# Norms with 1/rms kept in PSUM, squares added one tile late, biases on ScalarE, and other banks and held weights in the output products

## The chip, the cores and the metric

The kernel runs on one core of a Trainium2 chip. The metric is the device time of one execution in microseconds. Five engines work side by side, each on a queue of its own in program order: TensorE (PE in the profile) for matmuls, VectorE (DVE), ScalarE (ACT), GpSimd (POOL), and SyncE (SP), which issues most DMAs. They meet through semaphores. TensorE writes its products to banks of PSUM; the kernel's tiles there hold 128 x 512 fp32 numbers (a `wide` one is two of them), and a tile's place is written anew once its last reader is through.

## What is computed

The reference is one step of a diffusion backbone of two layers on 128 prompt tokens and 512 latent tokens, with 1024 features. Cut to what matters here:

```python
for l in range(DEPTH):
    hp = modulate(rmsnorm(xp, norm_mix_g[l]), sp_m, sc_m)
    hs = modulate(rmsnorm(xs, norm_mix_g[l]), ss_m, scs_m)
    # even layer: SSD scan and attention, @ w_out; odd layer: RG-LRU, @ w_out
    xp = xp + gp_m * out_p
    xs = xs + gs_m * out_s
    xp = xp + gp_f * conv_ffn(modulate(rmsnorm(xp, norm_ffn_g[l]), sp_f, sc_f), *fw)
    xs = xs + gs_f * conv_ffn(modulate(rmsnorm(xs, norm_ffn_g[l]), ss_f, scs_f), *fw)
def rmsnorm(x, g):
    return x * lax.rsqrt(jnp.mean(x * x, axis=-1, keepdims=True) + EPS) * g
def modulate(h, shift, scale):
    return h * (1.0 + scale) + shift
def conv_ffn(h, w_up, conv_w, conv_b, w_down):
    u = dwconv_centred(h @ w_up, conv_w, conv_b)
    val, g = jnp.split(u, 2, axis=-1)
    return (jax.nn.silu(g) * val) @ w_down
```

Shift, scale and gate (the modulation) come from a product of two conditioning vectors with `w_mod`. All is fp32.

## The kernel before

**Layout.** Activations lie transposed: features on the 128 partitions in 8 tiles (KD = 8), tokens in 644 columns (128 prompt, 4 empty, 512 latent). Each fp32 product is made of three matmuls on operands that are split in a high and a low part (`mm3`, lines 470 to 472): high by high, low by high, high by low. So every weight is loaded by DMA (`wraw`, three buffers), cast by ScalarE to its high part (line 112) and subtracted by GpSimd in pieces of 256 columns for its low part (line 117). These standard slots hold three weights. In the last products of a stage further weights are "held": they are split into a pool of their own (lines 126 and 129) that is opened when buffers of the stage before are given back. In the FFN most up weights come in pairs whose sums and differences VectorE makes (lines 139 to 142).

**Order.** The order on each engine is that of the program. It is written by hand: every product of one weight tile counts as a tick, and `after(n, f)` puts f n ticks later. NORM_A, NORM_B, NORM_D and NORM_F say after how many ticks the steps of a norm come.

**Output products.** `out_parts` (line 644) makes the eight tiles of an output product, first for the columns of part 0 and then of part 1 (388 and 256 columns, in B 260 and 384). Each tile is read from PSUM by VectorE, times the gate, and added to the residual X (`add_part`, line 317 as X<-..., the helper `fma`). `bank` or `wide_banks` hands out the PSUM banks: in A two of 512 columns in turn (tag "g"), elsewhere three pairs. Weights are split ahead by AHEAD = 3, but no further than the eighth. This is used four times: A is layer 0's output product (line 1440), B and D the last down products of the two FFNs (line 1636), C that of the RG-LRU (line 1852).

**Norms.** `square_acc` (lines 533 to 537) squares each new tile of X on ScalarE and adds the square on VectorE to `sq`. When a part is done, `norm_part` puts into the stream of products: the sums over features by TensorE (line 554), mean and eps by VectorE (line 556), the power -1/2 by GpSimd (line 558), a product that spreads 1/rms of a token over all partitions (line 565), and ScalarE's copy of it from PSUM to `sq` (line 569). Then `gen` makes tile after tile: VectorE multiplies 1/rms, the scale and X (`fma`, one operation for each stream of tokens), ScalarE adds the shift (line 600) and casts to the high part `hhi` (line 603; for even tiles lines 600 and 603 are one operation). `low` makes the low part `hlo`: for odd tiles by GpSimd (line 69), for even ones by VectorE, which adds the shift again (`fma`). In the two FFN norms the rows are kept (`keep`, `k.full`). From them `sums` (lines 1498 to 1502) makes the sums for paired weights; there VectorE first adds the shift to the even tiles, and GpSimd makes one of four differences.

**Modulation.** `make_mod` spreads the product with `w_mod` over the first half of the kernel, up to 1108 us. Each `M.step` (line 332, eight small matmuls) writes a PSUM bank that VectorE adds to `macc` (lines 338 and 340); after eight steps two transposes (line 347) and VectorE's line 352 finish a part. `small()` (line 545) gives the bank: where the plan of PSUM is "narrow" always "m", else `mtile()` hands out "m" and "o" in turn. FFN 0 isn't narrow and has 45 such steps; the norms' sums and rows take their banks from `mtile()` too.

## Time and profile before

| | us |
|---|---|
| median of 3 runs | 2131.27 |
| lowest, highest | 2123.99, 2131.78 |
| the profiled execution | 2128.0 |
| its span, first to last instruction | 2126.2 |

The profiled execution took 1.8 us more than its span. By stretches of the span:

| stretch | us | TensorE busy | VectorE busy | clock |
|---|---|---|---|---|
| 720 to 801.4 (A, output products of layer 0) | 81.4 | 70.08 | 38.56 | 0.96 |
| 801.4 to 860 (head of FFN 0) | 58.6 | 48.56 | 46.76 | 0.90 |
| 860 to 1272 (FFN 0) | 412.0 | 403.87 | 313.15 | 0.99 |
| 1272 to 1322.3 (B, last down products of FFN 0) | 50.3 | 35.34 | 34.92 | 0.87 |
| 1322.3 to 1550 (RG-LRU) | 227.7 | 179.50 | 188.84 | 0.87 |
| 1550 to 1617.6 (C, output products of the RG-LRU) | 67.6 | 52.62 | 39.17 | 0.85 |
| 1617.6 to 1680 (head of FFN 1) | 62.4 | 48.89 | 46.31 | 0.86 |
| 1680 to 2069 (FFN 1) | 389.0 | 372.73 | 302.76 | 0.99 |
| 2069 to 2126.2 (D, last down products and outputs) | 57.2 | 40.73 | 27.77 | 0.90 |

Busy times are in us. The clock is the mean that was granted to TensorE, 1.00 for the higher of its two levels (2.4 GHz) and 0.50 for the lower (1.2 GHz). TensorE is busy 1891.4 us in all (89%), VectorE 1467.3 (69%), GpSimd 1208.1 (57%) and ScalarE 964.2 (45%). Where TensorE's busy time is near the stretch's length, the products set the time; elsewhere what ends its idle time does.

### The profile page before, as it was taken

Reading aid. Unit: us, or ns where it says so; the run is one execution under the profiler, and the core shown is the slowest. Engines: PE = TensorE matmul, PEld = TensorE weight load, DVE = VectorE, ACT = ScalarE, POOL = GpSimd, SP = SyncE. Lnnn points to the kernel's source line nnn. Section 1 sums busy time; section 2 is a strip of 40 time slices with the busy share of each in tenths; the row PEclk is TensorE's granted clock in tenths of the full one; section 3 lists DMA queues with packets and bytes.
Section 4 is the critical chain, followed back from the end, with each engine's and each line's share of the span. In section 5 each row is a group of like instructions: output and inputs, shape, how many; then the busy total and the mean of one; then the engine's idle time right before and its main releaser. Section 6 shows DMA issues by size and latency. Waiting matters only on the chain.

```text
span 2126.2 us, 33767 instructions
## 1 busy us (share of the span) xinstructions
PE 1891.4 (89%) x12665; PEld 1735.7 (82%) x12665; DVE 1467.3 (69%) x2486; ACT 964.2 (45%) x1671; POOL 1208.1 (57%) x1542
## 2 busy tenths in 40 slices
PE   6878889999999988999999997977778799999997
PEld 4767768888888878799889997977678799999986
DVE  3477755656664357687777876788857778777874
ACT  3454444454553334343333444766724444343445
POOL 3335454333343535466666775688755577766772
PEclk9889999999999999999999998989789899999998
DMA  9545432121113431444542222111111122222221
GB/s 267 165 156 164 149 110 63 49 54 48 49 45 124 131 117 64 136 130 153 178 145 70 60 84 79 53 39 45 40 50 41 37 79 82 86 76 70 60 85 65
DMA packets 255578, 196.60 MB, mean 92 GB/s; under 512 B 13837, under 2 KB 233816, under 8 KB 255288
## 3 DMA queue, kind: packets, MB, share of 16 engines
q1 hardware_dynamic: 252664, 184.59, 28.9%
q0 software_dynamic: 2528, 7.13, 1.4%
q8 instruction: 100, 1.64, 0.3%
q10 hardware_dynamic: 224, 2.73, 0.3%
q14 instruction: 62, 0.51, 0.1%
HBM read 187.50 MB, written 6.92 MB: 91 GB/s over the span
## 4 chain that ended last, share of the span: by engine, by line
PE 36%; DVE 11%; POOL 9%; ACT 4%; issue 4%; DMA 4%; POOLq 0%; DVEq 0%; ACTq 0%; SPq 0%
PE wide L470 10%; PE wide L471 10%; PE wide L472 10%; POOL t L69 4%; POOL wlo L117 4%; DMA wraw<-in_ffn_w_up_dram 4%; DVE ft L317 2%; PE mt L332 1%; PE gh L470 1%; DVE X L317 1%; PE gh L471 1%; PE gh L472 1%; DVE wsum L141 1%; DVE wraw L140 1%; DVE wsum L139 1%
## 5 line engine op out<-in xcount | busy, mean ns | idle before, releaser
L117 POOL TENSOR_TENSOR wlo<-wraw,whi 128x256 fp32r<-128x256 f32 (+1 forms) x845 | 715.7, 875 | 544.7 <-ACT whi L112 476.8
L470 PE MATMUL wide<-hhi,whi 128*128 128x322 f32 (+4 forms) x1072 | 352.5, 329 | 49.5 <-DVE X L317 23.0
L471 PE MATMUL wide<-hlo,whi 128*128 128x322 f32 (+4 forms) x1072 | 345.8, 323 | 3.7 <-DVE hlo L511 3.4
L472 PE MATMUL wide<-hhi,wlo 128*128 128x322 f32 (+4 forms) x1072 | 343.1, 320 | 0.0
L112 ACT CAST whi<-wraw 128x1024 fp32r<-128x1024 f32 (+2 forms) x263 | 220.1, 839 | 150.4 <-PE wide L472 71.9
L470 PEld LDWEIGHTS wide<-hhi,whi 128*128 128x128 f32 x1072 | 213.2, 199 | 66.4 <-issue 21.6
L470 PE MATMUL gh<-hhi,whi 128*128 128x322 f32 (+3 forms) x704 | 236.7, 336 | 9.1 <-ACT zt L1160 8.6
L471 PE MATMUL gh<-hlo,whi 128*128 128x322 f32 (+3 forms) x704 | 221.2, 314 | 1.3 <-DVE hlo L511 1.0
L472 PE MATMUL gh<-hhi,wlo 128*128 128x322 f32 (+3 forms) x704 | 220.5, 313 | 0.0
L471 PEld LDWEIGHTS wide<-hlo,whi 128*128 128x128 f32 x1072 | 212.6, 198 | 6.1 <-DVE hlo L511 5.3
L472 PEld LDWEIGHTS wide<-hhi,wlo 128*128 128x128 f32 x1072 | 212.4, 198 | 0.0
L470 PE MATMUL wide<-hidh,whi 128*128 128x322 f32 (+4 forms) x624 | 199.7, 320 | 2.2 <-DVE ft L1584 2.2
L471 PE MATMUL wide<-hidl,whi 128*128 128x322 f32 (+4 forms) x624 | 195.5, 313 | 1.6 <-DVE hidl L511 1.6
L472 PE MATMUL wide<-hidh,wlo 128*128 128x322 f32 (+4 forms) x624 | 195.4, 313 | 0.0
L317 DVE SCALAR_TENSOR_TENSOR ft<-ft,PC 128x643 f32<-128x643 f32 x160 | 168.2, 1072 | 37.3 <-ACT ft L1526 35.3
L470 PEld LDWEIGHTS gh<-hhi,whi 128*128 128x128 f32 (+1 forms) x704 | 134.0, 190 | 34.7 <-issue 21.3
L1526 ACT ACTIVATE ft<-ft,PC 128x644 f32<-128x644 f32 x80 | 74.0, 927 | 144.4 <-DVE ft L1591 133.4
L317 DVE SCALAR_TENSOR_TENSOR X<-wide,modc,X 128x128 f32<-128x128 f32 (+3 forms) x264 | 123.5, 511 | 19.8 <-PE wide L472 19.8
L471 PEld LDWEIGHTS gh<-hlo,whi 128*128 128x128 f32 (+1 forms) x704 | 133.8, 190 | 2.4 <-DVE hlo L511 1.2
L472 PEld LDWEIGHTS gh<-hhi,wlo 128*128 128x128 f32 (+1 forms) x704 | 133.6, 190 | 0.6
L470 PEld LDWEIGHTS wide<-hidh,whi 128*128 128x128 f32 x624 | 118.7, 190 | 15.9 <-issue 7.0
L112 ACT CAST shi<-wsum 128x512 fp32r<-128x512 f32 x120 | 72.8, 617 | 124.3 <-DVE wsum L141 111.4
(386 smaller groups left out, 4676.4 us busy)
## 6 DMA issues: line engine op xcount, KB each, us to landing
wraw<-in_ffn_w_up_dram SPq DMA_DIRECT2D x88, 512.0 KB
mraw<-in_w_mod_dram SPq DMA_DIRECT2D x80, 512.0 KB
wraw<-in_ssd_attn_w_in_dram SPq DMA_DIRECT2D x42, 512.0 KB
wraw<-in_ffn_w_down_dram SPq DMA_DIRECT2D x96, 192.0 KB
E<-ad SPq DMA_DIRECT2D x16, 640.0 KB
mraw<-in_w_mod_dram SPq DMA_DIRECT2D x32, 256.0 KB
wraw<-in_ssd_attn_w_out_dram SPq DMA_DIRECT2D x16, 512.0 KB
wraw<-in_lru_w_in_dram SPq DMA_DIRECT2D x16, 512.0 KB
```

The costliest lines, as they stand in the source:

```text
L69: getattr(eng, op)(out[:, c], a[:, c], b[:, c])
L112: self.nc.scalar.copy(hi, src)
L117: low.tensor_sub(lo[:, q], src[:, q], hi[:, q].bitcast(F32))
L139: v.tensor_sub(s[:, 1], a[:, :4], b[:, :4])
L140: v.tensor_add(b[:, :4], b[:, :4], b[:, 4:])
L141: v.tensor_sub(s[:, 0], b[:, :4], a[:, :4])
L317: nc.vector.scalar_tensor_tensor(out, in0, scalar, in1, op0=op0, op1=op1, **kw)
L332: nc.tensor.matmul(m[32 * j:32 * j + 32, :256], scp[:, kt, :], raw[:, j * 256:(j + 1) * 256], start=half is None or kt == 0, stop=half is ...
L470: nc.tensor.matmul(ps[:whi.shape[-1], p0:p0 + c1 - c0], whi, xhi[:, c0:c1], start=start, stop=False)
L471: nc.tensor.matmul(ps[:whi.shape[-1], p0:p0 + c1 - c0], whi, xlo[:, c0:c1], start=False, stop=False)
L472: nc.tensor.matmul(ps[:whi.shape[-1], p0:p0 + c1 - c0], wlo, xhi[:, c0:c1], start=False, stop=stop)
L1526: after(at, lambda: nc.scalar.activation(out, u, AF.Identity, scale=par(cw, 2 * NF + t), bias=par(cb, t)))
```

## The change

1. The rows of 1/rms stay in PSUM, in bank "o"; `gen` reads them there (`box.m`), and ScalarE's copies go. The norm of the SSD output keeps the copies.
2. `square_acc` adds the square of the tile before, instead of its own; `rstd_cols` adds the last one.
3. With `keep`, every tile gets its shift on ScalarE in place and is then cast; the low part of an even tile is one subtraction on VectorE. The additions of shifts in `sums` go, and GpSimd's difference moves to VectorE.
4. In A, two of three pairs of tiles get wide banks.
5. The number of weights in standard slots is given for each of the four places: 2 in A (six held), 0 in B (eight held), 3 in C and D as before. The bound at the eighth weight goes, so that the next stage's first weights are split during part 0 if slots are free.
6. `small()` and `rstd_cols` always take bank "m".

```diff
@@ -40,7 +40,7 @@
 FF_CHUNKS = (3, 3, 3, 3, 3, 3, 4)
 N_PLAIN = 2
 PIECE = 256
-N_STD = 3
+N_STD = (2, 0, 3, 3)
 N_WAIT = 1
 AHEAD = 3
 N_HID, N_FT = 4, 5
@@ -392,7 +392,7 @@
             add_w(w_in, 0, 8, b + 128 * h)
     for half in range(2):
         for n in range(8):
-            add_w(w_out, 1024 * half, 8, 128 * n, kind=held(n, N_STD) if half else None)
+            add_w(w_out, 1024 * half, 8, 128 * n, kind=held(n, N_STD[0]) if half else None)
 
     def early(c):
         return 1 if c else FF_CHUNKS[c]
@@ -412,7 +412,7 @@
 
         def downs(c, last=False):
             for n in range(8):
-                add_w(dn, 128 * starts[c], FF_CHUNKS[c], 128 * n, kind=held(n, N_STD) if last else None)
+                add_w(dn, 128 * starts[c], FF_CHUNKS[c], 128 * n, kind=held(n, N_STD[1 + 2 * l]) if last else None)
         for c, n in enumerate(FF_CHUNKS):
             ups(c, 0, early(c))
             if c:
@@ -543,11 +553,12 @@
         return k.psum.tile([128, 512], F32, name="mt", tag=tag, bufs=1)
 
     def small():
-        return mtile("m" if k.narrow else None)
+        return mtile("m")
 
     def rstd_cols(chunks):
 
-        m = mtile()
+        add_square()
+        m = mtile("m")
         n = len(chunks)
         for i, c in enumerate(chunks):
             c0, c1 = CHUNKS[c]
@@ -558,19 +569,15 @@
         nc.gpsimd.tensor_tensor(r, v, expo[:, :n], op=OP.pow)
         return r
 
-    def rstd_rows(r, hf):
-
-        m = mtile()
+    def rstd_rows(r, hf, tag):
+
+        m = mtile(tag)
         for i in range(len(k.cut.chunks[hf])):
             nc.tensor.matmul(m[:, 128 * i:128 * i + 128], r[:, i:i + 1].to_broadcast([128, 128]), ident,
                              start=True, stop=True)
-        at = 0
-        for _, c0, c1 in k.cut.segs[hf]:
-            nc.scalar.copy(k.sq[:, c0:c1], m[:, at:at + c1 - c0])
-            at += c1 - c0
+        return m
 
     def norm_part(hf, l, which, keep=None, then=None, at=NORM_B):
-
 
         box, ts = Core(), {}
         k.fresh[hf] = False
@@ -581,9 +588,12 @@
 
         def low(kt):
             t, h, lo = ts.pop(kt), hhi[kt], hlo[kt]
-            if kt % 2:
+            if kt % 2 or keep:
                 c = slice(*k.cut.parts[hf])
-                pieces(nc.gpsimd, "tensor_sub", lo[:, c], t[:, c], h[:, c].bitcast(F32))
+                if kt % 2:
+                    pieces(nc.gpsimd, "tensor_sub", lo[:, c], t[:, c], h[:, c].bitcast(F32))
+                else:
+                    nc.vector.tensor_sub(lo[:, c], t[:, c], h[:, c].bitcast(F32))
                 return
             for s, c0, c1 in segs:
                 B = modc[l][:, s, 24 * which + kt:24 * which + kt + 1]
@@ -594,11 +604,13 @@
                 t = ts[kt] = keep[kt] if keep else k.tmp.tile([128, NT], F32, name="sqt", tag=k.sq_tag, bufs=k.n_sqt)
                 if hf == 0 and (kt % 2 or keep):
                     nc.vector.memset(t[:, NP:S0], 0.0)
+                whole, at = kt % 2 or keep, 0
                 for s, c0, c1 in segs:
                     A, B = acol[l][which][:, s, kt:kt + 1], modc[l][:, s, 24 * which + kt:24 * which + kt + 1]
-                    fma(t[:, c0:c1], k.sq[:, c0:c1], A, X[:, kt, c0:c1], op0=OP.mult, op1=OP.mult)
-                    nc.scalar.activation((t if kt % 2 else hhi[kt])[:, c0:c1], t[:, c0:c1], AF.Identity, bias=B)
-                if kt % 2:
+                    fma(t[:, c0:c1], box.m[:, at:at + c1 - c0], A, X[:, kt, c0:c1], op0=OP.mult, op1=OP.mult)
+                    nc.scalar.activation((t if whole else hhi[kt])[:, c0:c1], t[:, c0:c1], AF.Identity, bias=B)
+                    at += c1 - c0
+                if whole:
                     c = slice(*k.cut.parts[hf])
                     nc.scalar.copy(hhi[kt][:, c], t[:, c])
             if kt:
@@ -608,7 +620,10 @@
                 then()
 
         after(at[0], cols)
-        after(at[0] + at[1], lambda: rstd_rows(box.r, hf))
+        def rows():
+            box.m = rstd_rows(box.r, hf, "o")
+
+        after(at[0] + at[1], rows)
         for kt in range(KD + 1):
             after(at[0] + at[1] + at[2] + at[3] * kt, lambda kt=kt: gen(kt))
 
@@ -641,7 +656,7 @@
                     M.step()
                     W.ahead()
 
-    def out_parts(xs, evac, then, banks, first, ready, n_std=N_STD):
+    def out_parts(xs, evac, then, banks, first, ready, n_std):
 
 
         ws, base = [], W.next
@@ -668,7 +683,7 @@
                 for j, f in enumerate(late):
                     f()
                     if j == len(late) - 1:
-                        W.upto(min(base + batch[-1][-1] + AHEAD, base + 7))
+                        W.upto(base + batch[-1][-1] + AHEAD)
                         break
                     for g in batch:
                         for i in g:
@@ -1369,7 +1384,10 @@
 
             def rows(rs):
                 for hf in range(2):
-                    rstd_rows(rs[hf], hf)
+                    m, at = rstd_rows(rs[hf], hf, "m"), 0
+                    for _, c0, c1 in k.cut.segs[hf]:
+                        nc.scalar.copy(k.sq[:, c0:c1], m[:, at:at + c1 - c0])
+                        at += c1 - c0
                 for t in range(KD):
                     after(5 * t + 5, lambda t=t: fma(X[:, t], X[:, t], par("ssd_g", t), k.sq, op0=OP.mult, op1=OP.mult))
             after(5 * KD + 8, lambda: after(12, lambda rs=[rstd_cols(c) for c in k.cut.chunks]: rows(rs)))
@@ -1412,7 +1430,14 @@
                 k.given.clear()
             half_unit(H, out, ready=lambda c0: k.n or c0 in k.given, cuts=k.cut.parts if k.n == 7 else HALVES)
 
+        turn = []
+
         def bank(n):
+
+            if n == 2:
+                turn.append(0)
+            if n == 2 and len(turn) % 3:
+                return wide_banks(2)
             return [k.psum.tile([128, 512], F32, name="gh", tag="g", bufs=2) for _ in range(n)]
 
         def ready():
@@ -1437,7 +1462,7 @@
                 until(lambda: k.fresh[0])
         until(lambda: len(k.given) == 2)
         hctx = ExitStack()
-        out_parts(H, evac, then, bank, [[0], [1]], [ready])
+        out_parts(H, evac, then, bank, [[0], [1]], [ready], N_STD[0])
         W.over = None
         hctx.close()
 
@@ -1492,12 +1517,8 @@
             def sums(kt):
 
                 x, y = full[kt], full[kt + 4]
-                if kt % 2 == 0:
-                    for i, t in ((kt, x), (kt + 4, y)):
-                        for s, cols in STREAMS:
-                            nc.vector.tensor_scalar(t[:, cols], t[:, cols], modc[l][:, s, 24 + i:25 + i], None, op0=OP.add)
                 nc.vector.tensor_sub(x[:, L], x[:, R], x[:, L])
-                nc.gpsimd.tensor_sub(x[:, R], y[:, R], x[:, R])
+                nc.vector.tensor_sub(x[:, R], y[:, R], x[:, R])
                 nc.vector.tensor_sub(y[:, R], y[:, R], x[:, L])
                 nc.vector.tensor_sub(y[:, L], y[:, L], y[:, R])
 
@@ -1633,7 +1654,7 @@
                         norm_part(0, 1, 0, at=NORM_D)
                     else:
                         until(lambda: k.fresh[0])
-                out_parts(xs, evac, then, wide_banks, [[0, 1], [2, 3], [4, 5]], [ready])
+                out_parts(xs, evac, then, wide_banks, [[0, 1], [2, 3], [4, 5]], [ready], N_STD[1 + 2 * l])
                 W.over = None
 
             def ups(c, j0, j1):
@@ -1849,7 +1870,7 @@
                     norm_part(0, 1, 1, k.full, at=NORM_A)
                 else:
                     until(lambda: k.fresh[0])
-            out_parts(H, evac, then, wide_banks, [[0, 1], [2]], [lambda: until(lambda: k.scanned > 6 and k.n_given == 14), ready], 3)
+            out_parts(H, evac, then, wide_banks, [[0, 1], [2]], [lambda: until(lambda: k.scanned > 6 and k.n_given == 14), ready], N_STD[2])
             W.over = None
             hctx.close()
             m = mtile()
```

**Where the order changes.** VectorE in C, the last two norm tiles of part 0 (`full` is the kept tile, `acol` the scale, `modc` the shift, `mt` the bank with the rows). Before:

```order
1541 L596 MEMSET full 128x4
1542 L317 SCALAR_TENSOR_TENSOR full<-sq,acol_117,X 128x128
1543 L317 SCALAR_TENSOR_TENSOR full<-sq,acol_117,X 128x256
1544 L596 MEMSET full 128x4
1545 L317 SCALAR_TENSOR_TENSOR full<-sq,acol_117,X 128x128
1546 L317 SCALAR_TENSOR_TENSOR full<-sq,acol_117,X 128x256
1547 L317 SCALAR_TENSOR_TENSOR hlo_88<-full,modc_113,hhi_80 128x128
1548 L317 SCALAR_TENSOR_TENSOR hlo_88<-full,modc_113,hhi_80 128x256
```

After:

```order
1523 L606 MEMSET full 128x4
1524 L317 SCALAR_TENSOR_TENSOR full<-mt,acol_117,X 128x128
1525 L317 SCALAR_TENSOR_TENSOR full<-mt,acol_117,X 128x256
1526 L606 MEMSET full 128x4
1527 L317 SCALAR_TENSOR_TENSOR full<-mt,acol_117,X 128x128
1528 L317 SCALAR_TENSOR_TENSOR full<-mt,acol_117,X 128x256
1529 L596 TENSOR_TENSOR hlo_88<-full,hhi_80 128x388
```

The fma reads `mt` instead of `sq`, and one subtraction stands for two fma.

GpSimd in B, from the last split of a held weight on (`lo` is the low part of a held weight, `wlo` of a weight in a standard slot, `hlo` of the norm's output; a held weight of B has two pieces). Before:

```order
418 L129 TENSOR_TENSOR lo_12961<-wraw,hi_12960 128x256 x2
419 L558 TENSOR_TENSOR rstd<-msq,expo 128x2
420 L69 TENSOR_TENSOR hlo_83<-sqt,hhi_75 128x130 x2
421 L69 TENSOR_TENSOR hlo_85<-sqt,hhi_77 128x130 x2
422 L117 TENSOR_TENSOR wlo<-wraw,whi 128x256 x12
423 L69 TENSOR_TENSOR hlo_87<-sqt,hhi_79 128x130 x2
424 L69 TENSOR_TENSOR hlo_89<-sqt,hhi_81 128x130 x2
```

After:

```order
416 L129 TENSOR_TENSOR lo_12950<-wraw,hi_12949 128x256 x2
417 L117 TENSOR_TENSOR wlo<-wraw,whi 128x256 x12
418 L569 TENSOR_TENSOR rstd<-msq,expo 128x2
419 L69 TENSOR_TENSOR hlo_83<-sqt,hhi_75 128x130 x2
420 L69 TENSOR_TENSOR hlo_85<-sqt,hhi_77 128x130 x2
421 L69 TENSOR_TENSOR hlo_87<-sqt,hhi_79 128x130 x2
422 L69 TENSOR_TENSOR hlo_89<-sqt,hhi_81 128x130 x2
```

The twelve pieces of the LRU's first three weights moved from behind the norm's power and two tiles to ahead of both. Right ahead of the rows shown stand four more such rows of `lo` in the old order and seven in the new.

ScalarE in B, its casts and squares of part 0 (`sq` and `sqt` are squares, `whi` the high part of a standard weight, `hi` of a held one). Before:

```order
802 L126 CAST hi_12939<-wraw 128x512
803 L507 CAST hidh<-ft 128x644
804 L126 CAST hi_12960<-wraw 128x512
805 L533 ACTIVATE sq<-X 128x260
806 L536 ACTIVATE sqt<-X 128x260 x7
807 L533 ACTIVATE sq<-X 128x384
808 L536 ACTIVATE sqt<-X 128x384
```

After:

```order
806 L126 CAST hi_12928<-wraw 128x512
807 L507 CAST hidh<-ft 128x644
808 L126 CAST hi_12949<-wraw 128x512
809 L112 CAST whi<-wraw 128x1024
810 L534 ACTIVATE sq<-X 128x260
811 L537 ACTIVATE sqt<-X 128x260 x5
812 L112 CAST whi<-wraw 128x1024 x2
813 L537 ACTIVATE sqt<-X 128x260 x2
814 L534 ACTIVATE sq<-X 128x384
815 L537 ACTIVATE sqt<-X 128x384
```

One cast of an LRU weight stands ahead of the first square and two stand ahead of the last two.

## Rows read from the trace of the kernel before

**Rows 1.** Windows by stage: us, each engine's busy time (instructions), clock, DMA.

```profile
860.00:1272.00 412.00, 403.87 (x2813) 376.05 (x2812) 313.15 (x469) 162.86 (x253) 277.01 (x339) 0.99 0.40 122
```

**Rows 2.** Timeline, TensorE, A: start, us, instruction, [idle before <-releaser].

```profile
745.44 0.42 PE L470 MATMUL gh<-hhi,hi 128*128 128x388 f32 x1 [1.29 <-DVE X L317]
...
792.98 0.58 PE L470 MATMUL gh<-hhi,hi 128*128 128x256 f32 x1 [5.69 <-DVE X L317]
```

**Rows 3.** Timeline, VectorE, norm operations of A (same columns).

```profile
785.17 0.95 DVE L317 SCALAR_TENSOR_TENSOR full<-sq,acol,X 128x256 f32<-128x256 f32 x1
...
786.05 1.70 DVE L317 SCALAR_TENSOR_TENSOR hlo<-full,modc,hhi 128x128 fp32r<-128x128 f32 x2
...
792.46 0.47 DVE L317 SCALAR_TENSOR_TENSOR X<-gh,modc,X 128x256 f32<-128x256 f32 x1
...
810.49 0.87 DVE L317 SCALAR_TENSOR_TENSOR full<-sq,acol,X 128x256 f32<-128x256 f32 x2
```

**Rows 4.** C: TensorE's gap (timeline); VectorE by line, 1592 to 1618.

```profile
1617.59 0.67 PE L470 MATMUL wide<-hhi,whi 128*128 128x388 f32 x1 [6.78 <-DVE lt L1858]
...
L317 DVE SCALAR_TENSOR_TENSOR full<-sq,acol,X 128x256 f32<-128x256 f32 x8 | 5.6, 701 | 0.0
...
L317 DVE SCALAR_TENSOR_TENSOR full<-sq,acol,X 128x128 f32<-128x128 f32 x8 | 4.5, 563 | 2.3 <-ACT sq L569 2.3
...
L537 DVE TENSOR_TENSOR sq<-sq,sqt 128x256 f32<-128x256 f32 x7 | 3.1, 436 | 4.5 <-ACT sqt L536 4.5
...
L317 DVE SCALAR_TENSOR_TENSOR hlo<-full,modc,hhi 128x256 fp32r<-128x256 f32 x4 | 2.9, 714 | 0.0
```

**Rows 5.** Timeline, B: TensorE, GpSimd twice, VectorE.

```profile
1322.27 0.56 PE L470 MATMUL wide<-hhi,whi 128*128 128x260 f32 x1 [8.14 <-DVE X L317]
...
1276.87 10.41 POOL L129 TENSOR_TENSOR lo<-wraw,hi 128x256 fp32r<-128x256 f32 x10
...
1298.59 0.70 POOL L558 TENSOR_TENSOR rstd<-msq,expo 128x2 f32<-128x2 f32 x1 [11.31 <-DVE msq L556]
...
1320.93 0.66 DVE L537 TENSOR_TENSOR sq<-sq,sqt 128x384 f32<-128x384 f32 x1 [0.80 <-ACT sqt L536]
```

**Rows 6.** Windows just after the gaps of A and C (columns of Rows 1).

```profile
794.00:796.00 2.00, 2.00 (x11) 2.00 (x11) 0.66 (x2) 0.42 (x1) 0.85 (x2) 0.50 0.72 217
...
1619.00:1621.00 2.00, 2.00 (x9) 2.00 (x9) 0.16 (x1) 0.00 (x0) 0.18 (x1) 0.50 0.00 0
```

**Rows 7.** Timeline, GpSimd, A: one row of splits.

```profile
782.78 9.47 POOL L117 TENSOR_TENSOR wlo<-wraw,whi 128x256 fp32r<-128x256 f32 x12 [0.86 <-ACT whi L112]
```

**Rows 8.** Line 537: VectorE idle before it until (us, times).

```profile
  ACT sqt L536: 38.5, 57
```

**Rows 9.** Timeline, VectorE in FFN 0's head, TensorE in FFN 1's.

```profile
812.18 1.75 DVE L1498 TENSOR_SCALAR full<-full,modc 128x128 f32<-128x128 f32 x4
...
815.33 0.49 DVE L1501 TENSOR_TENSOR full<-full 128x322 f32<-128x322 f32 x1 [1.00 <-POOL full L1500]
...
1658.53 0.64 PE L470 MATMUL wide<-t24h,shi 128*128 128x322 f32 x1 [4.62 <-ACT shi L112]
...
1676.88 0.60 PE L470 MATMUL wide<-hhi,shi 128*128 128x322 f32 x1 [4.52 <-DVE ft L1579]
```

**Rows 10.** Timeline, modulation steps of FFN 0 (TensorE) and their reads (VectorE).

```profile
825.30 0.64 PE L332 MATMUL mt<-mraw,scp 128*32 128x256 f32 x8
...
833.11 0.41 DVE L340 TENSOR_TENSOR macc<-macc,mt 128x256 f32<-128x256 f32 x1
...
878.66 0.64 PE L332 MATMUL mt<-mraw,scp 128*32 128x256 f32 x8
...
878.76 0.24 DVE L352 TENSOR_TENSOR modc<-mt,PC 128x8 f32<-128x8 f32 x2 [1.22 <-PE mt L347]
...
1104.61 0.64 PE L332 MATMUL mt<-mraw,scp 128*32 128x256 f32 x8
...
1105.29 0.41 DVE L340 TENSOR_TENSOR macc<-macc,mt 128x256 f32<-128x256 f32 x1
```

13 lines of the change are left out of this document (10 added, 3 removed).

## The prediction

> **What bounds the kernel now.** I read the stretches first, then in each stretch TensorE's idle time and what ended it, then the engine that ended it. The 40 slices show TensorE 89% busy, so the middle of the kernel's two feed-forward blocks cannot be helped by edits to norms: in the first of them TensorE is busy 403.9 of 412 us [rows 1]. Whatever stalls TensorE there is lost whole, and whatever the change can win lies in the stretches between: A (output products of layer 0, 720 to 801), the head of FFN 0 (801 to 860), B (last down products of FFN 0, 1272 to 1322), C (output products of the LRU, 1550 to 1618), the head of FFN 1 (1618 to 1680) and D (the end, from 2069). In these TensorE waits for VectorE, in two ways. First, a bank of PSUM isn't read yet: 1.29 us, twice, and 5.69 us in A [rows 2]. The 5.69 us end when VectorE gets to the evacuation at 792.46, behind a row of norm operations [rows 3]. Second, all norm work is over late: 6.78 us in C [rows 4] and 8.14 us in B [rows 5]. Each of these gaps costs a second time: TensorE comes back at 0.50 of its clock, the lower of its two levels, in 794 to 796 and in 1619 to 1621 [rows 6].
>
> Why VectorE is slow there is the main reading. `full<-sq,acol,X` on 256 columns takes 0.95 us at 785.17 and 0.87 for two (0.44 each) at 810.49; the pair that writes `hlo` takes 1.70 [rows 3]. What differs is GpSimd, which splits three weights from 782.78, twelve pieces in 9.47 us [rows 7]. But `X<-gh,modc,X`, whose first operand lies in PSUM, takes 0.47 at 792.46, while GpSimd runs `hlo` pieces. So two operands in SBUF are slowed beside GpSimd and one in PSUM with one in SBUF is not.
>
> **The rows of 1/rms in PSUM.** The fma of the norms gets a PSUM operand. Beside GpSimd, an operation of 256 columns should fall from 0.95 to 0.47; in C the eight of them average 701 ns [rows 4]. The trace has no fma of this form with the row in PSUM; the bounds are 0.47 (that X row) and 0.95 (no change at all), and I take 0.47, since only the operand that lies in PSUM differs. For reads of PSUM by VectorE the Trainium skill (Perfetto Trace Analysis, Optimizing Scalar/DVE Operations) gives an overhead about 65 ns above that of SBUF. The row of 0.47 against 0.44 shows less than half of that; by the page 16 operations in a stretch would cost 1 us more, which changes no sign. ScalarE also loses its copies of the rows.
>
> **Squares one tile late.** VectorE's add no longer stands right behind ScalarE's square: 38.5 us of waits, 57 times, vanish from VectorE [rows 8]. In A's first half they stood beside products, where TensorE was the slower one; in the second halves and in D VectorE's loop is what TensorE waits for. The last add of a part is flushed ahead of the sums and costs there what it cost before.
>
> **Biases by ScalarE.** For the two FFN norms the pair that wrote an even `hlo` (1.70 beside GpSimd) becomes one subtraction. It has two operands in SBUF, so I take 1.0 (one such operation beside GpSimd, as at 785.17). In the sums that follow, the additions of biases go: 1.75 us at 812.18 and four shorter ones a second time, I take 3 per FFN. The subtraction by GpSimd goes to VectorE: a round trip made VectorE wait 1.00 us before 815.33, and its own subtraction of that size takes 0.49 [rows 9]; four such per FFN make 4 x (1.00 - 0.49) = 2.0. Together VectorE is 5 us shorter in each head. ScalarE gets a cast more for each even tile; it was busy half of these stretches, which hides it unless it becomes the bound of the norm's loop (below).
>
> **A.** Gaps 2 x 1.29 and 5.69 go, since products of two pairs get other banks and VectorE's stretch from 784 to 792 is nearly halved; the half clock behind the 5.69 (some 4 us at half speed) gives 2. Against it, one more weight is held, and its split comes after the attention's buffers are given back: 4 pieces of 0.79 us [rows 7], between 0 and 3.2, I take 0.5 because two such weights lie ahead of it. A: -2.6 - 5.7 - 2.0 + 0.5 = **-10** (-13 to -5).
>
> **C and the head of FFN 1.** The 6.78 us gap: VectorE has 25 us of unbroken work before it. Of that go some 2 us on the 256-column fma, as much on those of 128, 2 on `hlo`, and 4.5 of waits for squares [rows 4]. That is 10, more than the gap, so what is left is TensorE's own evacuation; I take 5.6 of it and 2.5 of half clock. In the head, gaps of 4.62 and 4.52 wait for casts and an evacuation that stand behind VectorE's sums [rows 9]: of the 5 us that VectorE saves I take 4. Together **-12** (-15 to -7).
>
> **B.** No weight of the last down products is in the standard slots any more; all eight are held, and the LRU's first three weights are split in the first half. GpSimd then has 16 pieces of held weights and 12 of the LRU's before the power of the norm, where it had 10 and an idle wait of 11.31 before 1298.59 [rows 5]. Ten pieces took 10.41 from 1276.87, so 28 of them, 12 at 0.79, end near 1303: the norm starts up to 4 us later. It then runs without GpSimd beside it and without a wait for a square per tile (0.80 at the longest [rows 5]), which I estimate at 5.5 over eight tiles. I take **-1.5** (-6 to +6).
>
> **D.** The loop of evacuations loses a wait per tile (38.5 / 57 = 0.68 on average [rows 8]), 16 in all, but most of them sit beside products, so I take a quarter: **-2.5** (-4 to 0).
>
> **The bank of the small products.** This part speaks against the change. In FFN 0 the steps of the modulation product (line 332) used two banks in turn; now all use one. A step then waits until VectorE has read the step before it. I set each step against the end of that read in the trace. At 825.30 the step before is added from 833.11 to 833.52: 8.2 us too late [rows 10]; a neighbour lacks 7.1 and another 0.9. In the middle of FFN 0 ten of 41 steps lack something: from 0.34 at 878.66 (read until 879.00) to 1.09 at 1104.61 (read until 1105.70), 15.4 us in all [rows 10]. A stall moves later steps too, which takes some lags away, so I take **+10** (+5 to +14). In the head VectorE is 5 us earlier by its shorter sums, and TensorE idles later there anyhow, so I set the head at **-2** (-5 to +6) with both. The Trainium skill (Perfetto Trace Analysis, Matmuls) has independent matmul groups rotate through PSUM banks so that evacuation overlaps; the lags above are what it costs to stop that, and the same rule is for A's extra banks.
>
> **Sum.** -10 - 12 - 1.5 - 2.5 + 10 - 2 = -18. The profiled execution took 2128.0 us, so 2110 for such a one; the median of the runs is 3.3 above it, so **2113**.
>
> **Rivals.** One: the lags are paid in full, 31.6 us over 45 steps (0.70 each), against gains of 28 without that bank: +3.6, about 2135, no change. For it speaks that TensorE works in order and has no slack in the middle [rows 1]; against it that several lags stand in a row behind one late add, of which only the first counts. Two, the slower side, is the same bank with every step held up: beyond 0.87 us a step the 45 steps cost 39, more than the gains plus 0.5%. At the last step's 1.09 they cost 49: 2152. Against it: 31 steps in the middle lack nothing. Three: the order of queues in B decides. ScalarE's casts of LRU weights stand ahead of squares, and GpSimd's 12 pieces ahead of the power; if their DMA is late, squares, norm and then the LRU's first products wait: +6 instead of -1.5, about 2120. Four: the change doesn't give what it says, because ScalarE becomes the bound of the norms' loop (a third operation for the even tiles) in place of VectorE: A and C give half, 2124. Five: better than forecast. VectorE's shorter work makes the reads of the steps earlier too, the bank costs 3, and A and C give their far ends: 2099.
>
> **Chances.** Forecast 0.47, full lags 0.16, every step held up 0.07, B's queues 0.08, ScalarE the bound 0.07, better 0.15. The range 2094 to 2135 leaves out the held-up steps and the far half of the better case. A measurement of this kernel can tell about 0.5% from no change, 10.7 us: faster is below 2120.6. That has the forecast, the better case and half of B's: 0.68; within 0.5% 0.23; slower 0.09.
>
> **What would show it.** Right, if line 317's fma of 256 columns shows 0.47 to 0.5 beside GpSimd, the additions of squares follow with no wait for ScalarE, and the gaps of 5.69 and 6.78 are under 2. If the modulation steps show waits for line 338 to 352 of some 10 us in FFN 0, the bank's term is right. In B the power should start 3 to 4 us later in its stage. The prediction is wrong if the middle of FFN 0 lasts as long as before, if it lasts over 16 us longer, or if the fma from PSUM stays at 0.9 beside GpSimd.

## The result and the profile after

The changed kernel takes 2114.24 us (median of 7 runs, 2110.73 to 2120.58); the kernel before takes 2127.93 (median of 7 runs). The ratio is 0.9934, with a 95% interval of 0.9917 to 0.9950: 0.7% faster. The span of the profiled execution falls from 2126.2 to 2108.9 us.

TensorE executes 12665 matmuls in both kernels, so a stage can be timed from one matmul to another by their places in TensorE's order. (Where an edit swaps neighbours, that is off by some tenths.) "B, part 0" and "part 1" are the two column parts, and "first LRU" is the work on the first weights behind them.

| stage, us | before | after | difference | forecast |
|---|---|---|---|---|
| A | 80.4 | 70.9 | -9.5 | -10 |
| head of FFN 0 | 59.6 | 58.2 | -1.4 | -2 |
| middle of FFN 0 | 411.0 | 426.0 | +15.1 | +10 |
| B, part 0 | 29.1 | 31.8 | +2.7 | |
| B, part 1 | 22.9 | 16.2 | -6.7 | -1.5 (both parts) |
| first LRU | 17.1 | 14.7 | -2.3 | (with B) |
| C | 67.2 | 62.1 | -5.1 | -12 (with the head) |
| head of FFN 1 | 62.2 | 57.1 | -5.1 | |
| D | 57.1 | 53.1 | -4.0 | -2.5 |

These make -16.3; stages that no edit touches make the rest of the span's change. Such stages vary by one or two microseconds from one kernel to the next (the middle of FFN 1 from 388.5 to 391.1, the SSD by 6), and D varied from 51.7 to 54.6 among kernels in which its edits were the same. A difference below 2 us in one stage is no finding here, and D's is only known within 3.

**The middle of FFN 0** is the one place that lost. The windows of the changed kernel, the first over the stretch of [rows 1], the other two just ahead of and behind one stall (columns as there):

```profile
847.50:1274.50 427.00, 409.38 (x2813) 381.24 (x2811) 311.51 (x470) 162.94 (x251) 272.70 (x336) 0.98 0.39 117
...
903.00:905.90 2.90, 2.90 (x21) 2.74 (x19) 2.43 (x4) 1.10 (x2) 2.90 (x4) 1.00 0.04 11
...
909.50:911.50 2.00, 2.00 (x12) 1.19 (x13) 1.15 (x4) 2.00 (x3) 2.00 (x5) 0.50 0.00 0
```

TensorE idles 17.6 us instead of 8.1, and it is busy 409.4 instead of 403.9, for the same number of matmuls. Waits ahead of the modulation steps make 11.8 us of that, in eight steps, where they made 0.7 in two. Four of TensorE's stalls there and in the head, and two reads they wait for (timeline: start, us, instruction, idle before and its releaser):

```profile
889.01 0.64 PE L332 MATMUL mt<-mraw,scp 128*32 128x256 f32 x8 [0.94 <-DVE macc L340]
...
909.48 1.08 PE L332 MATMUL mt<-mraw,scp 128*32 128x256 f32 x8 [3.49 <-issue]
...
909.14 0.23 DVE L352 TENSOR_TENSOR modc<-mt,PC 128x8 f32<-128x8 f32 x2
...
962.23 1.08 PE L332 MATMUL mt<-mraw,scp 128*32 128x256 f32 x8 [3.84 <-issue]
...
820.00 1.08 PE L332 MATMUL mt<-mraw,scp 128*32 128x256 f32 x8 [5.71 <-DVE macc L340]
...
819.53 0.41 DVE L340 TENSOR_TENSOR macc<-macc,mt 128x256 f32<-128x256 f32 x1
```

At 909.48 the step starts when VectorE's line 352, 909.14 to 909.37, has read the bank that the two transposes before it wrote; the profile has "issue" for it and names no releaser, so that this read ended the wait is read off the times. The step at 962.23 stands behind the same line's read in the same way (961.91 to 962.14). The one at 820.00 is the head's, behind the addition at 819.53. Behind the long stalls the step takes 1.08 us instead of 0.64, and the window 909.5 to 911.5 has a granted clock of 0.50.

**A and C** lost the gaps that the prediction names. The longest one left in A, and the one at A's end (timeline):

```profile
749.06 0.64 PE L332 MATMUL mt<-mraw,scp 128*32 128x256 f32 x8 [1.94 <-DMA mraw<-in_w_mod_dram]
...
790.38 0.41 PE L470 MATMUL wide<-hhi,whi 128*128 128x388 f32 x1 [0.67 <-DVE X L317]
```

The 1.94 us are a modulation step's wait for its own weights, which no term of the prediction has. TensorE at the end of C (timeline):

```profile
1607.81 0.41 PE L470 MATMUL wide<-hhi,whi 128*128 128x388 f32 x1 [1.42 <-DVE lt L1879]
```

VectorE by line in the stretch that answers to [rows 4] (1586 to 1608; out<-in, xcount | busy, mean ns | idle before, what ended most of it):

```profile
L317 DVE SCALAR_TENSOR_TENSOR full<-mt,acol,X 128x256 f32<-128x256 f32 x8 | 3.8, 475 | 0.0
...
L317 DVE SCALAR_TENSOR_TENSOR full<-mt,acol,X 128x128 f32<-128x128 f32 x8 | 2.8, 344 | 2.0 <-PE mt L576 2.0
...
L547 DVE TENSOR_TENSOR sq<-sq,sqt 128x256 f32<-128x256 f32 x7 | 4.1, 580 | 0.0
...
L596 DVE TENSOR_TENSOR hlo<-full,hhi 128x388 fp32r<-128x388 f32 x4 | 3.0, 760 | 2.8 <-ACT hhi L615 2.8
```

The gap of 6.78 is 1.42 now. The fma of 256 columns takes 475 ns and that of 128 columns 344, where they averaged 701 and 563; in both kernels GpSimd's splits run beside three of the eight of 256 columns. The additions of squares wait for nothing, but take 580 ns instead of 436. VectorE now waits for ScalarE's cast, 2.8 us in four subtractions. Over the whole kernel, the waits of the squares' addition fall from the 38.5 us of [rows 8]; line 547 is the old line 537:

```profile
  ACT sqt L537: 7.1, 11
```

**GpSimd in B** (timeline), and two of TensorE's waits there, to be set beside [rows 5]:

```profile
1279.10 4.32 POOL L129 TENSOR_TENSOR lo<-wraw,hi 128x256 fp32r<-128x256 f32 x6 [1.37 <-issue]
...
1284.17 9.88 POOL L129 TENSOR_TENSOR lo<-wraw,hi 128x256 fp32r<-128x256 f32 x10 [0.75 <-ACT hi L126]
...
1295.19 3.18 POOL L117 TENSOR_TENSOR wlo<-wraw,whi 128x256 fp32r<-128x256 f32 x4 [1.14 <-ACT whi L112]
...
1300.65 6.15 POOL L117 TENSOR_TENSOR wlo<-wraw,whi 128x256 fp32r<-128x256 f32 x8 [2.28 <-ACT whi L112]
...
1306.75 0.70 POOL L569 TENSOR_TENSOR rstd<-msq,expo 128x2 f32<-128x2 f32 x1
...
1279.02 0.58 PE L470 MATMUL wide<-hidh,hi 128*128 128x260 f32 x1 [3.92 <-ACT hi L126]
...
1321.18 0.36 PE L470 MATMUL wide<-hhi,whi 128*128 128x260 f32 x1 [0.80 <-DVE X L317]
```

Sixteen held pieces and the LRU's twelve stand ahead of the power, GpSimd waits 1.14 and 2.28 us for ScalarE's casts among them, and TensorE waits 3.92 us for the first held weight. Counted from the start of part 0, the power comes at 33.1 us instead of 27.5. The gap at the end of B is 0.80 instead of 8.14.

### The profile page after: what moved, and what is told of

Read it like the earlier page. It is cut to its first block, busy times and chain, and to the rows that moved or that the text cites. A ratio compares the mean times of both kernels' runs of the same rounds, so it can differ in the third digit from the quotient of the medians.

```text
span 2108.9 us, 33780 instructions
## 1 busy us (share of the span) xinstructions
PE 1890.9 (90%) x12665; PEld 1734.8 (82%) x12665; DVE 1445.7 (69%) x2470; ACT 966.6 (46%) x1678; POOL 1200.2 (57%) x1534
## 4 chain that ended last, share of the span: by engine, by line
PE 36%; DVE 10%; POOL 9%; issue 4%; DMA 4%; ACT 4%; POOLq 0%; DVEq 0%; SPq 0%; ACTq 0%
PE wide L470 11%; PE wide L471 10%; PE wide L472 10%; POOL wlo L117 4%; POOL t L69 4%; DMA wraw<-in_ffn_w_up_dram 4%; DVE ft L317 2%; PE mt L332 1%; DVE wsum L141 1%; DVE wraw L140 1%; DVE wsum L139 1%; PE gh L470 1%; DVE X L317 1%; DVE wsum L142 1%; PE gh L471 1%
## 5 line engine op out<-in xcount | busy, mean ns | idle before, releaser
L112 ACT CAST whi<-wraw 128x1024 fp32r<-128x1024 f32 (+1 forms) x259 | 217.3, 841 | 169.2 <-PE wide L472 77.5
L470 PE MATMUL wide<-hidh,whi 128*128 128x322 f32 (+2 forms) x600 | 192.2, 320 | 1.1 <-DVE ft L1605 1.1
L471 PE MATMUL wide<-hidl,whi 128*128 128x322 f32 (+2 forms) x600 | 187.7, 313 | 0.8 <-DVE hidl L511 0.8
L472 PE MATMUL wide<-hidh,wlo 128*128 128x322 f32 (+2 forms) x600 | 187.6, 313 | 0.0
L317 DVE SCALAR_TENSOR_TENSOR X<-wide,modc,X 128x128 f32<-128x128 f32 (+3 forms) x276 | 128.3, 507 | 34.4 <-PE wide L472 34.4
L470 PEld LDWEIGHTS wide<-hidh,whi 128*128 128x128 f32 x600 | 114.4, 191 | 14.9 <-issue 8.6
```

The source lines that it names most:

```text
L112: self.nc.scalar.copy(hi, src)
L317: nc.vector.scalar_tensor_tensor(out, in0, scalar, in1, op0=op0, op1=op1, **kw)
L470: nc.tensor.matmul(ps[:whi.shape[-1], p0:p0 + c1 - c0], whi, xhi[:, c0:c1], start=start, stop=False)
L471: nc.tensor.matmul(ps[:whi.shape[-1], p0:p0 + c1 - c0], whi, xlo[:, c0:c1], start=False, stop=False)
L472: nc.tensor.matmul(ps[:whi.shape[-1], p0:p0 + c1 - c0], wlo, xhi[:, c0:c1], start=False, stop=stop)
```

## Experiments

All kernels but two start from the changed kernel; the other two from the one before. Stage times are measured as in the table above. Kernels that ran once have one time only. Stage times are those of one profile each, so the bound of 2 us stands.

**One bank or two.** First the undoing:

```diff
     def small():
-        return mtile("m")
+        return mtile("m" if k.narrow or not all(k.fresh) else None)
```

> The changed kernel, but the modulation steps of FFN 0 again use banks m and o in turn whenever no norm holds its rows in o. Theory (the single bank costs FFN 0's middle all of its 15 us, by waits of about 10 us and by the half clock behind them): the middle (up to the last down products) lasts 411 us again instead of 426, its head 1 to 4 us less than in the changed kernel, and the whole takes 2095 to 2100 us. Rival (the lost time is the weights' DMAs and GpSimd's queue moved by the edits, and the waits on the bank only stand where another wait would): the middle stays above 420 us and the whole within 5 us of the changed kernel's 2114.

Measured: 2099.51 us (median of 4), ratio to before 0.9873 (0.9853 to 0.9893). The middle lasts 409.6 us, the head 57.0. Then the same edit alone, put into the kernel before:

```diff
     def small():
-        return mtile("m" if k.narrow else None)
+        return mtile("m")
```

> The kernel before with one edit: small() always gives bank m. Theory (the single bank alone costs it): the middle of FFN 0 lasts 423 to 428 us instead of 411, the head up to 6 more, the whole 2140 to 2148. Rival (other edits lost the time there): the middle stays within 4 us of 411 and the whole within 6 us of before.

Measured: 2146.11 us, ratio 1.0085 (1.0067 to 1.0104): slower than before. The middle lasts 429.6 us, the head 60.3. The windows over the stretch of [rows 1], of the two-bank kernel and of the one-bank kernel:

```profile
851.20:1261.80 410.60, 403.32 (x2812) 375.94 (x2812) 312.56 (x470) 162.07 (x251) 274.37 (x336) 0.99 0.40 122
```

```profile
859.10:1289.70 430.60, 409.69 (x2812) 381.31 (x2812) 314.26 (x469) 163.83 (x253) 273.47 (x339) 0.97 0.39 117
```

Both agree with the theory, but for a middle 1.6 us longer than it allowed in the second. The bank alone costs 15 to 19 us. With two banks idle and busy time are 7.3 and 403.3, about as before; with one they are 20.9 and 409.7. Of the price, 6 us is busy time: matmuls at the lower clock.

**Rows of 1/rms in SBUF again**, copied by ScalarE:

```diff
-            box.m = rstd_rows(box.r, hf, "o")
+            m, at = rstd_rows(box.r, hf, "o"), 0
+            for _, c0, c1 in segs:
+                nc.scalar.copy(k.sq[:, c0:c1], m[:, at:at + c1 - c0])
+                at += c1 - c0
...
-                    fma(t[:, c0:c1], box.m[:, at:at + c1 - c0], A, X[:, kt, c0:c1], op0=OP.mult, op1=OP.mult)
+                    fma(t[:, c0:c1], k.sq[:, c0:c1], A, X[:, kt, c0:c1], op0=OP.mult, op1=OP.mult)
```

> The changed kernel, but ScalarE copies 1/rms to SBUF again and the norms' fma reads it there. Theory (two operands in SBUF are slowed beside GpSimd): in C the fma of 256 columns averages 0.65 to 0.75 us instead of 0.475, TensorE's gap before FFN 1 grows from 1.4 to 3 to 5 us, and the whole is 3 to 7 us longer. Rival (VectorE has room by then, so the operand doesn't matter): gap and whole within 2 us.

Measured: 2118.34 us. C lasts 62.1 us, as with the rows in PSUM; A is 0.8 longer, B's part 1 and the first LRU products 0.6 each. VectorE by line in C:

```profile
L317 DVE SCALAR_TENSOR_TENSOR full<-sq,acol,X 128x256 f32<-128x256 f32 x8 | 5.1, 642 | 0.0
```

TensorE's gap at the end of C (timeline):

```profile
1616.17 0.42 PE L470 MATMUL wide<-hhi,whi 128*128 128x388 f32 x1 [1.52 <-DVE lt L1882]
```

The operation's price is as the theory had it: 642 ns against 475. The end of C is as the rival had it: 1.52 us of gap against 1.42. VectorE has room in C by then, so the operand doesn't set the time. This result counts against my theory. (The whole, 4.1 us above the changed kernel's median, lies in the theory's range, but it is one run, and in its profile 5.4 us of the difference stand ahead of A, where kernels vary by as much.)

**Squares at once:**

```diff
-            add_square()
             k.square = sq, t
+            add_square()
```

> The changed kernel, but each square is added right behind its own. By stages the changed kernel won 5.1 us in C, 9 in B after part 0, 4.0 in D. Theory (the late square is the edit that closes the gaps at the ends of parts): C is 3 to 6 us longer, B's second half 3 to 6, D 2 to 4, A 0 to 2; the whole 8 to 16 us longer than 2114. Rival (rows in PSUM and biases on ScalarE closed them): C and B within 2 us of the changed kernel's, only D longer.

Measured: 2129.31 us, beside 2129.66 for the kernel before on the same chip. A +0.1, head of FFN 0 +2.9, B +2.5 and +2.7, first LRU +1.8, C +2.0, head of FFN 1 +2.2, D +2.5. The total, A and D are the theory's; in C and in B's part 1 it asked for 3 to 6 and got 2.0 and 2.7, little more than the bound of 2. The gap at the end of C (timeline), and the window behind it:

```profile
1622.50 0.66 PE L470 MATMUL wide<-hhi,whi 128*128 128x388 f32 x1 [3.66 <-DVE lt L1879]
...
1622.50:1624.50 2.00, 2.00 (x6) 2.00 (x7) 0.00 (x0) 0.00 (x0) 0.11 (x1) 0.50 0.27 78
```

It is 3.66, between the 1.42 of the changed kernel and the 6.78 of before. The heads had not been named in the expectation. In FFN 0's the rows of 1/rms come 2.9 us later behind the head's start. In FFN 1's TensorE idles no longer than in the changed kernel (10.2 us against 10.7); it is busy 49.0 us against 46.1 for the same products, at the lower clock behind that gap.

**Both: rows in SBUF and squares at once** (the two edits above):

> The changed kernel without two edits: rows of 1/rms in SBUF and squares added at once. With the rows alone in SBUF, C's fma averaged 642 ns against 475, yet C stayed at 62.1 us. Theory (either edit gives VectorE enough room in C, so only both together show): C is 65 to 68 us, nearly the 67.2 of before, and more than the sum of the two single removals. Rival (they add up): C is longer by the same as with squares at once alone, within 1 us.

Measured: 2138.87 us. C lasts 66.6 us, 4.5 more than in the changed kernel, where the two single removals give 0.0 and 2.0. TensorE at the end of C:

```profile
1631.28 0.66 PE L470 MATMUL wide<-hhi,whi 128*128 128x388 f32 x1 [6.15 <-DVE lt L1882]
```

The gap of 6.15 is nearly the old one, and C is as the theory had it. So in C either edit gives VectorE most of the room, and neither has a price of its own that could be read from the other's absence.

**Late squares alone**, in the kernel before (`add_square` is that of the change):

```diff
         if n == 0:
+            add_square()
             nc.scalar.activation(sq, X[:, n, c0:c1], AF.Square)
         else:
             t = k.tmp.tile([128, NT], F32, name="sqt", tag=k.sq_tag, bufs=k.n_sqt)[:, c0:c1]
             nc.scalar.activation(t, X[:, n, c0:c1], AF.Square)
+            add_square()
+            k.square = sq, t
+
+    k.square = None
+
+    def add_square():
+
+        if k.square:
+            (sq, t), k.square = k.square, None
             nc.vector.tensor_add(sq, sq, t)
...
     def rstd_cols(chunks):
 
+        add_square()
         m = mtile()
```

> The kernel before with the late squares alone. Taking them out of the changed kernel lengthened it by 15 us (heads 5, B 5, C 2, D 2.5, first LRU products 2). Theory (they carry most of the change's gain by themselves): 2112 to 2118, of it C 3 to 5 us shorter, D 2 to 4, B 4 to 6. Rival (they need the rows in PSUM, since otherwise VectorE stays behind beside GpSimd): 2120 to 2126.

Measured: 2112.18 us (median of 4), ratio 0.9925 (0.9906 to 0.9945): this one edit is as fast as the whole change. (With two banks the whole change took 2099.51, so its one bank takes back about what the edits other than late squares win.) A is 3.5 us shorter, B 3.5 and 4.7, C 4.5, D 3.8; the first LRU products are 4.0 longer, the heads the same within 1. Waits of the addition over the kernel (us, times):

```profile
  ACT sqt L537: 7.4, 11
```

The gap at the end of C (timeline):

```profile
1604.82 0.41 PE L470 MATMUL wide<-hhi,whi 128*128 128x388 f32 x1 [1.87 <-DVE lt L1869]
```

The gap falls to 1.87 with fma that still have two operands in SBUF. The theory holds in the total, in C and in D. B's two parts win 8.2 us instead of 4 to 6, of which the first LRU products give 4.0 back; A's 3.5 it had not named, and the heads, which lost in the removal, win nothing here. Where the 4.0 go can be read in the same trace (timeline, ScalarE and TensorE):

```profile
1313.51 0.52 ACT L537 ACTIVATE sqt<-X 128x384 f32<-128x384 f32 x1 [4.43 <-POOL hlo L69]
...
1315.52 1.46 PE L565 MATMUL mt<-ones,sq 128*128 128x16 f32 x6 [3.21 <-DVE sq L547]
```

The squares and the norm's tiles share the places of `sqt`. The square before the last of part 1 waits until GpSimd has read such a tile for `hlo`, which stands behind the twelve pieces of the LRU's weights (1302.96 to 1312.60). The sums of part 1 wait for it, and TensorE idles 3.21 us among the first LRU products. Before, it had no such wait there; it had stood 8.14 us ahead of them, where it stands 4.45 now.

**The old banks in A:**

```diff
-            if n == 2 and len(turn) % 3:
+            if False:
```

> The changed kernel, but A's products use the two old banks in turn. Theory (of A's 9.6 us, the two 1.29 and most of 5.69 with its half clock come from the added banks, since without them a product waits for an evacuation that stands behind norm work): A is 4 to 8 us longer. Rival (VectorE's norm work is so short now that banks come free in time): A is longer by the two 1.29 alone, 2 to 3 us.

Measured: 2113.34 us, with A 5.1 us longer and the other stages together 2.4 shorter than in the changed kernel's profile. In A the gap of [rows 2] comes back only in part:

```profile
746.22 0.42 PE L470 MATMUL gh<-hhi,hi 128*128 128x388 f32 x1 [1.29 <-DVE X L317]
...
784.96 0.38 PE L470 MATMUL gh<-hhi,hi 128*128 128x256 f32 x1 [1.43 <-DVE X L317]
```

The gaps of 1.29 (two of them) and 1.43 make 4.0 of the 5.1. So the stage answers as the theory said, but 5.69 became 1.43 without any added bank: VectorE's shorter stretch, late squares included, took the rest. With late squares alone A won 3.5. The total is no evidence, since it is one run.

**The old biases:**

```diff
-            if kt % 2 or keep:
+            if kt % 2:
...
-                whole, at = kt % 2 or keep, 0
+                whole, at = kt % 2, 0
...
+                if kt % 2 == 0:
+                    for i, t in ((kt, x), (kt + 4, y)):
+                        for s, cols in STREAMS:
+                            nc.vector.tensor_scalar(t[:, cols], t[:, cols], modc[l][:, s, 24 + i:25 + i], None, op0=OP.add)
                 nc.vector.tensor_sub(x[:, L], x[:, R], x[:, L])
-                nc.vector.tensor_sub(x[:, R], y[:, R], x[:, R])
+                nc.gpsimd.tensor_sub(x[:, R], y[:, R], x[:, R])
```

> The changed kernel, but with the old biases: even low parts by two operations of VectorE, the shifts of even tiles added by VectorE in the sums, one difference on GpSimd. Theory (FFN 1's head won its 5.0 us by these alone, FFN 0's head as much, which its bank took back): each head is 4 to 6 us longer, C and A 0 to 2, the whole 8 to 14. Rival (the heads were won by an earlier norm): heads within 2 us.

Measured: 2112.07 us. The heads are 2.1 and 1.9 us longer, C 0.8 shorter, A the same: some 2 us a head, the rival's bound, against the 4 to 6 of the theory, and nothing in the total that could be told. Part of the reason can be read in the changed kernel, where the sums' subtractions are all VectorE's (timeline, two in FFN 0's head and two in FFN 1's):

```profile
814.26 0.92 DVE L1520 TENSOR_TENSOR full<-full 128x322 f32<-128x322 f32 x1
...
816.06 0.90 DVE L1522 TENSOR_TENSOR full<-full 128x322 f32<-128x322 f32 x1
...
1619.51 0.49 DVE L1521 TENSOR_TENSOR full<-full 128x322 f32<-128x322 f32 x1
...
1623.08 0.49 DVE L1520 TENSOR_TENSOR full<-full 128x322 f32<-128x322 f32 x1
```

A subtraction of 322 columns, with its two operands in SBUF, takes 0.49 us when GpSimd is idle (1623.08). Beside GpSimd five of the 16 in each head take 0.8 to 0.9, among them all four of the third group; the one at 1619.51 doesn't, though a piece of GpSimd's runs from 1619.54 to 1620.60. Even so VectorE's time on the sums of FFN 1, waits included, falls from 15.0 us to 10.6. TensorE gets less of it (timeline, the kernel before, the changed one twice, the one with the old biases twice):

```profile
1651.89 0.39 PE L470 MATMUL wide<-hhi,whi 128*128 128x322 f32 x1 [2.20 <-DVE ft L317]
...
1643.49 0.64 PE L470 MATMUL wide<-t24h,shi 128*128 128x322 f32 x1 [4.21 <-ACT shi L112]
...
1661.84 0.61 PE L470 MATMUL wide<-hhi,shi 128*128 128x322 f32 x1 [4.55 <-DVE ft L1600]
...
1641.67 0.39 PE L470 MATMUL wide<-hhi,whi 128*128 128x322 f32 x1 [1.68 <-DVE ft L317]
...
1648.31 0.64 PE L470 MATMUL wide<-t24h,shi 128*128 128x322 f32 x1 [4.61 <-ACT shi L112]
```

The gaps of 4.62 and 4.52 [rows 9] are 4.21 and 4.55 in the changed kernel. What goes is the wait of 2.20 us ahead of them, and with the old biases 1.68 of it is back. With the new ones the sums also start later: 11.2 us behind the head's start against 9.9.

**Held weights in B.** Three standard slots again, with the old bound:

```diff
-N_STD = (2, 0, 3, 3)
+N_STD = (2, 3, 3, 3)
...
-                            W.upto(base + i + AHEAD)
+                            W.upto(min(base + i + AHEAD, base + 7))
...
-                        W.upto(base + batch[-1][-1] + AHEAD)
+                        W.upto(min(base + batch[-1][-1] + AHEAD, base + 7))
```

> The changed kernel with three of B's weights in standard slots again and the old bound on splitting ahead. From the last down products of FFN 0 to the first LRU products the change lost 4.9 us in part 0 and won 9 after it. Theory (part 0's loss is the held weights that come late; what was won later is the late squares and the rows in PSUM, which stand without the held weights): B is 3 to 5 us shorter than in the changed kernel. Rival (the later gain is the LRU's splits being out of the way of the norm): part 0 is 5 shorter, part 1 5 to 8 longer, so B is as long or up to 3 us longer.

Measured: 2109.57 us. Part 0 takes 24.4 us, 7.4 less; part 1 takes 16.6, 0.5 more; the first LRU products take 19.9, 5.2 more. GpSimd's power and its twelve pieces, and TensorE in the LRU's first products:

```profile
1298.71 0.70 POOL L569 TENSOR_TENSOR rstd<-msq,expo 128x2 f32<-128x2 f32 x1 [7.15 <-DVE msq L567]
...
1308.16 9.40 POOL L117 TENSOR_TENSOR wlo<-wraw,whi 128x256 fp32r<-128x256 f32 x12 [2.58 <-issue]
...
1315.60 0.56 PE L470 MATMUL wide<-hhi,whi 128*128 128x260 f32 x1 [2.94 <-DVE X L317]
...
1320.43 0.82 PE L565 MATMUL mt<-ones,sq 128*128 128x16 f32 x3 [3.19 <-DVE sq L547]
```

Neither expectation fits. Part 1 didn't need the LRU's splits out of its way (against the rival), but the first LRU products did (which the theory had not asked for): the twelve pieces end at 1317.56, the last `hlo` behind them, a square of part 1 waits 4.42 us for that as with late squares alone, and TensorE waits 2.94 and 3.19 us. From the start of B the sum is 1.8 us less, which is no finding. Three kernels with two banks for the modulation steps tell whether there is a better number. With two, one and three standard weights in B (the last with the old bound on splitting ahead):

```diff
-N_STD = (2, 0, 3, 3)
+N_STD = (2, 2, 3, 3)
```

> The changed kernel with two banks for the modulation steps, and two of B's weights in standard slots instead of none (one LRU weight is then split early, as in A). Eight held weights cost part 0 of B some 7 us and save the first LRU products 5. Theory (both follow from GpSimd's queue, so a middle number gets some of each): B's part 0 lasts 26 to 29 us, the first LRU products 15 to 18, B to the LRU 1 to 4 us less than with either end; 2095 to 2098 in all. Rival (the two costs trade one for one at every number): within 1.5 us of the two-bank kernel's B, 2098 to 2100.

```diff
-N_STD = (2, 0, 3, 3)
+N_STD = (2, 1, 3, 3)
```

> As the one with two standard weights, but with one (two LRU weights split early). Theory: part 0 of B 28 to 31 us, the first LRU products 14.7 to 16, 0 to 3 us less than with none; 2096 to 2099. Rival: one for one, 2098 to 2100.

```diff
-N_STD = (2, 0, 3, 3)
+N_STD = (2, 3, 3, 3)
```

> The changed kernel with two banks for the modulation steps and B's three standard weights as before. One look at the change without its held weights in B was 1.5 to 5 us shorter than the change. Theory (held weights in B bring nothing): 2096 to 2099. Rival (one for one): 2098 to 2101.

| standard weights in B | us | ratio to before (95%) | part 0 | part 1 | first LRU | sum |
|---|---|---|---|---|---|---|
| 0 (two banks, above) | 2099.51 | 0.9873 (0.9853 to 0.9893) | 31.7 | 16.1 | 14.7 | 62.5 |
| 1 | 2095.72 | 0.9848 (0.9829 to 0.9867) | 29.3 | 15.3 | 17.2 | 61.8 |
| 2 | 2097.82 | 0.9862 (0.9837 to 0.9888) | 27.1 | 18.9 | 16.1 | 62.2 |
| 3 (old bound) | 2095.77 | 0.9848 (0.9827 to 0.9868) | 24.4 | 16.3 | 20.9 | 61.5 |

What part 0 wins the first LRU products lose, nearly one for one; the sums lie within 1 us and the intervals overlap. The middle numbers give nothing of the 1 to 4 us that the theory had from two. In the stages the rival fits: the number of held weights in B moves the cost and doesn't remove it. The times with one and three standard weights lie 2 us below the rival's range, but the intervals don't tell them from the others. All four beat both kernels: the one before by 1.3 to 1.5%, the changed one by 0.7 to 0.9% of its median.

## Why the prediction was right and where it was not

The time is right: 2113 against 2114.24, faster, in the range. That it is so near is in part luck. The kernel before had a median of 2127.93 in more runs, 3.3 us below the one that I started from, and the gain was 13.7 us by medians (16.8 from the first matmul to the end) where I had 18. And the 5 us that the bank cost beyond my term were made good by B and D, which won 4.8 and 1.5 more than theirs.

The main reading held: all 32 fma of 256 columns that read PSUM take 0.47 to 0.48 us, the eight that stand wholly beside GpSimd too. But the row at 792.46 that it rested on could not show it by itself: an addition with both operands in SBUF, beside the same `hlo` pieces, took no longer than the 0.42 us of one at 799.03 with GpSimd idle. And the 0.44 us of [rows 3] for the operand in SBUF is half of a row of two operations that overlap; each takes 474 ns (the kernel before, timeline, and VectorE by line from 810.3 to 811.3):

```profile
793.41 0.43 DVE L537 TENSOR_TENSOR sq<-sq,sqt 128x256 f32<-128x256 f32 x1 [0.48 <-ACT sqt L536]
...
L317 DVE SCALAR_TENSOR_TENSOR full<-sq,acol,X 128x256 f32<-128x256 f32 x2 | 0.9, 474 | 0.0
```

- **The bank of the small products**: right in mechanism and place, and shown by two runs, the undoing and the edit alone. The size was off, +15.1 against +10, beyond my bound of +14. The step that failed is the price of a stall: I counted idle time, and of that TensorE had 9.5 us more, as estimated; but I had charged the half clock behind a gap only where a gap went (A, C), and not where gaps came. That is the other 5.5.
- **A**: -9.5 as forecast. The split was off. I had the banks and VectorE's shorter stretch remove the gaps together; without the added banks 4.0 us of gaps and 5.1 in all come back (in one run), so about half is the banks, and the rest norm work, late squares included, which had no term in A.
- **C and the head of FFN 1**: -10.1 against -12, but for other reasons. I gave C's end to fma, `hlo` and squares together. Late squares alone closed the gap but for 1.87, the other edits without them but for 3.66, and fma at 475 ns were worth nothing there once the squares were late. In the head TensorE idles 2.8 us less and is busy 2.5 us less (the half clock behind C's gap, which I had counted in C). I gave 4 us there to the shorter sums; some 2 is what they brought. The step that failed is the wait: the sums did get 4.4 of the 5 us shorter, though I had priced all their subtractions at 0.49 and five take 0.8 to 0.9, but the two gaps that I meant to shorten stayed, at 4.21 and 4.55, and only a wait of 2.20 ahead of them went.
- **Squares one tile late**: the mis-weighed edit. I let most of the 38.5 us lie beside products and gave it no term of its own outside B, C and D. By removal (one run) and by itself it is worth 15 to 16 us, as much as the whole change.
- **B**: -6.3 with the first LRU products, just beyond my bound of -6. The power came 5.6 us later in its stage, not 3 to 4: GpSimd waited 3.4 us for ScalarE's casts between the LRU's pieces. Part 1's 6.7 us don't come from GpSimd being out of the way, as I had it: with three standard weights and the splits behind the power, part 1 is as short (16.6 against 16.2), and late squares alone give 4.7 of it. What I had not counted is that the LRU's splits, done early, no longer stand ahead of its first products.
- **ScalarE as the bound**: it does make VectorE wait (2.8 us in C), but the gaps at the ends of A, B and C all end with VectorE.
- **Operands in PSUM and rotating banks**: The Trainium skill (Perfetto Trace Analysis, Optimizing Scalar/DVE Operations) gives VectorE an overhead of about 125 ns on PSUM against 60 on SBUF. No such difference shows here: the fma of 256 columns takes 475 ns with one operand in PSUM and 474 with both in SBUF and GpSimd idle. Where small products share one bank, the Trainium skill's rule that independent matmul groups rotate through PSUM banks (Perfetto Trace Analysis, Matmuls) is borne out by the two runs on the bank, at 15 to 19 us for the steps of FFN 0.
- **Slips in the working**: the better case adds up to 2100, not 2099, and the chances of faster to 0.66, not 0.68. The trace has 46 modulation steps in FFN 0, 42 of them in the middle, where I had 45 and 41.

What stays open: how much of D's 4.0 is real, and why the heads lose with squares at once but win nothing by late squares alone.
